# A GAT layer on one core: the row merges of both sorts as odd-even merges, with ends copied by ScalarE

## The chip, the cores and the metric

The kernel runs on one core of one Trainium2 chip. The metric is the device time of one execution in microseconds (us); the time of before is the median of three executions. Engine names are those of the profile: PE is TensorE's matmul side, PEld its weight loads, DVE is VectorE, ACT is ScalarE, POOL is GpSimd, SP is SyncE. L249 is line 249 of the kernel before.

## What is computed

The reference is a graph attention layer with 4096 nodes of 64 features, 50,000 random edges and 4 heads of 64 outputs. Cut to what matters:

```python
x_proj[h] = x @ weight[h]
score[h, e] = leaky_relu(x_proj[h, src[e]] . att_src[h] + x_proj[h, dst[e]] . att_dst[h], 0.2)
output[h, d] = sum over e with dst[e] == d of exp(score[h, e]) * x_proj[h, src[e]]
output[h, d] /= sum over the same e of exp(score[h, e]) + 1e-8
```

## The kernel before, in words

Edges are sorted on the chip so that the gather of source rows and the sums by destination become matmuls with one-hot matrices. The work has four stages.

**Keys.** The edge list arrives by DMA as 128 partitions of 391 columns (padded to L = 512 with a large key). DVE packs source and destination of an edge into one number (L944 to L949). Meanwhile POOL builds small constants (L97 to L178), among them two selector matrices `sel1` (four pieces of 128 columns, L168) and `sel2` (L171), and DVE waits for the first edges.

**First sort.** DVE sorts the rows, `Sorter.rows` (L266): merges of 2, 4, ... 512 columns, merge number k taking k steps. Each step is `Sorter.apart` (L220): compare columns h apart, write minima and maxima into the next of three or four buffers (`sA`, `sB`, `sZ`, `sY`). A step is three instructions: minima of one part of the columns, maxima of all, minima of the other part; the next step can begin on the first part while the last instruction is under way. Columns past 391 are padding, so the small merges work on 384 or 392 columns. Then `Sorter.runs` (L292) merges the rows of a run of four partitions: ACT multiplies by a sign (L301), DVE swaps partitions (L304) and joins (L307, L310), then nine column steps (a "crossing"), a 32 x 32 transposition (`turn`, L285), one or two steps, a transposition back, nine more steps. The result goes to HBM (L338).

During these steps ACT counts edges by source group: 16 passes of Sign with an accumulator (L345), whose sums over partitions PE forms with `sel1` (L355). The counts tell where each group's stretch begins. PE and ACT then prepare tables (`tables`, L485): transposes of x and of the weights, and attention scores of all nodes (L525, 128 small fp32 matmuls). `tables` is a generator; the calls of `next(rest)` decide where in each engine's queue its pieces stand.

**Second sort** (`group`, L452). POOL gathers four stretches per partition by indirect DMA (L445), two for the left 256 columns and two for the right. `Sorter.pairs` (L254) merges each half as soon as it is there, then `rows(9)` merges both into sorted rows of 512, and `runs` merges runs of eight partitions with two turns back and forth. ACT has 32 Sign passes here (L345, 13 of them queued ahead of `runs`, the rest behind the sign multiplication L301 and two casts L469). PE idles, so `busy` (L967) queues filler matmuls of 512 columns on it: one that waits for the 26th count (`WARM`), 12 more (`EARLY`), then the matmul of the counts (L355, `sel2`), which needs all 32, then 34 fillers (`LATER`). Behind them in PE's queue stands `spread` (L594), which copies the sorted fields of a partition to all partitions and which needs DVE's fields (L984, L985) cast by ACT (L986).

**Blocks.** For 32 blocks of 128 destinations: one-hot matrices by DVE (L615, L617), gathers by PE (L634 to L636), exponentials and evictions by ACT (L646, L648), weighted values by DVE (L668), sums by PE (L732), the projection and the store. The first block gets its indices by `spread`, later ones over HBM.

Instructions stand in the order in which the program lists them on each engine (the whole of it is scheduled by hand), so a waiting instruction holds up all that is behind it on its engine. The lines of `group` that fix the order here (the second part is `then`, called by `runs` behind the sign multiplication):

```python
        for f in todo[:SOON]:
            f()
        so.begin(raw)
        so.pairs(5)
        so.rows(9)
        ...
            for f in todo[SOON:]:
                f()
            if between:
                busy(EARLY, (sel2[:], sgn[:, WARM:WARM + 1]))
            st.ps = counts(pp, sgn, 8 * NI, [sel2[:]])
            if between:
                S.copy(out=adb[:, :, 0:P], in_=av(identb[:], 0, [0, ND], [1, P]))
                busy(LATER)
```

Of the kernel before, what the change touches and what calls it, by code (L numbers as in the profile page):

```python
# [11 lines left out]
P = 128  # L12
# [19 lines left out]
SOON = 13  # L32
WARM = 26
EARLY = 12
REST = 2
LATER = 34
# [14 lines left out]
def kernel(ctx: ExitStack, tc: tile.TileContext, x: bass.AP, edge_index: bass.AP,  # L51
# [48 lines left out]
    ident = cst.tile([P, P], F32)  # L100
    make_identity(nc, ident[:])
# [9 lines left out]

# [13 lines left out]
    p8 = bits("p8", 3, 15)  # L125
    p4 = bits("p4", 2, 31)
# [6 lines left out]
    ones = cst.tile([P, 1], F32)  # L133
# [32 lines left out]
    sel1 = cst.tile([P, SETS, P], F32)  # L166
# [3 lines left out]
    sel2 = cst.tile([P, P], F32)  # L170
    G.tensor_scalar(out=sel2[:], in0=av(ioF[:], 0, [0, 8], [1, 16]), scalar1=p8[:, 0:1], scalar2=None,  # L171
                    op0=OP.is_equal)
# [19 lines left out]
    long = cst.tile([P, SPANS], F32)  # L192
# [4 lines left out]
    class Sorter:  # L197


        def __init__(self, pool):  # L200
            self.a = [None, *(pool.tile([P, L], F32, name=n) for n in ("sA", "sB", "sZ", "sY"))]

        def begin(self, first):
            self.a[0] = first
            self.cur = 0

        def step(self, ring=4):
            s = self.a[self.cur]
            self.cur = self.cur % ring + 1
            return s, self.a[self.cur]  # L210
# [9 lines left out]
        def apart(self, j, width=L, cut=L // 2, right=False, at=0, mirror=False, opposed=False, ring=4, to=None, then=None):  # L220


            s, d = self.step(ring)
            d = to or d
# [8 lines left out]
            if right and n > 1:  # L233
                parts.reverse()
            for (o, *dims), op in ((parts[0], OP.min), (whole, OP.max), (parts[1], OP.min)):
                low = at + o
                top = op == OP.max
                if mirror:
                    turned = [*dims[:-1], [-1, dims[-1][1]]]
                    i0 = o % (2 * h)  # L240
                    out = av(d[:], low + h * top, *dims)
                    in0 = av(s[:], low + h * top, *dims)
                    in1 = av(s[:], low - i0 + 2 * h - 1 - i0 - h * top, *turned)
                else:
                    out, in0, in1 = av(d[:], low + h * top, *dims), av(s[:], low, *dims), av(s[:], low + h, *dims)
# [4 lines left out]
                if then:  # L250
                    then()
                    then = None

        def pairs(self, alone):  # L254

            k = 8
            was = self.cur
            for at in (0, L // 2):
                self.cur = was
                self.apart(k - 1, L // 2, at=at, mirror=True)  # L260
                for j in range(k - 2, k - 1 - alone, -1):
                    self.apart(j, L // 2, L // 4, True, at)
            for j in range(k - 1 - alone, -1, -1):
                self.apart(j)

        def rows(self, first, n=L, then=None):  # L266

            w8 = -(-n // 8) * 8
            w128 = n // 128 * 128 if n % 128 <= 8 else L
            for k in range(first, 10):  # L270
                w = w8 if k <= 3 else w128 if k <= 7 else L
                if k <= 7:
                    for j in range(k - 1, -1, -1):
                        self.apart(j, w, 256 if k == 7 else 192, mirror=j == k - 1, ring=3, then=then)
                        then = None
                        if k == 4 and j == 2 and w < w8:
                            V.tensor_copy(out=self.a[1][:, w:w8], in_=self.a[3][:, w:w8])
                else:
                    self.apart(k - 1, w, mirror=True)
                    for j in range(k - 2, -1, -1):  # L280
                        self.apart(j, w if j > 6 else w128 if j > 2 else w8, right=k == 9)
                if k == 7:
                    assert self.cur == 1

        def turn(self, parts):  # L285

            s, d = self.step()
            w = L // parts
            for i in reversed(range(parts)):
                V.transpose(out=d[:, i * w:(i + 1) * w], in_=s[:, i * w:(i + 1) * w])  # L290

        def runs(self, size, then, skey, to=None, fine=0, between=()):  # L292
# [6 lines left out]
            halves = (slice(L // 2, L), slice(0, L // 2))  # L299
            for c in halves:  # L300
                S.activation(out=y[:, c], in_=s[:, c], func=ACTF.Identity, scale=sig[:, 0:1])  # L301
            then()
            for c in reversed(halves):
                V.stream_shuffle(out=z[:, c], in_=s[:, c], mask=[p ^ 1 for p in range(32)])  # L304
            d = self.step()[1]
            for c in halves:
                V.scalar_tensor_tensor(out=d[:, c], in0=av(z[:], L - 1 - c.start, [-1, L // 2]), scalar=sig[:, 0:1],  # L307
                                       in1=y[:, c], op0=OP.mult, op1=OP.min)
            s, d = self.step()
            V.tensor_scalar(out=d[:], in0=s[:], scalar1=sj[0][:, 0:1], scalar2=None, op0=OP.mult)  # L310
            for m in range(1, levels):
                for j in range(8, -1, -1):
                    self.apart(j, right=True)
                self.turn(2)
                self.apart(m, right=True, opposed=True)
                for j in range(m - 1, -1, -1):
                    self.apart(j, right=True)
                self.turn(1)
            todo = list(between)
            for j in range(8, fine, -1):  # L320
# [3 lines left out]
                else:  # L324
                    self.apart(j, right=True)
# [776 lines left out]
```

## Time and profile before

| | |
|---|---|
| median of three executions | 259.68 us (259.49, 259.68, 260.8) |
| the profiled execution, its own time | 260.12 us |
| its span in the trace | 258.2 us |
| busy: PE / DVE / ACT / POOL | 201.1 / 242.4 / 200.0 / 48.7 us |
| first instruction to the end of the first sort's row steps | 0 to 35.4 us |
| crossings and turns of the first sort | 35.4 to 54.0 us |
| through HBM to the second sort | 54.0 to 60.7 us |
| second sort | 60.7 to 102.9 us |
| blocks | 102.9 to 258.2 us |

In a row of the timeline stand the start of the first instruction in us, the time from its start to the end of the last of the row, the engine, the line, the operation, what it writes and reads with shapes, and the number of instructions; in brackets, the idle time before it and what ended it. Instructions of DVE overlap a little at their ends, so what one costs in a stream is read from start to start. "span" is from the first instruction to the last; the execution's own time is 1.9 us more.

### The profile page before, as it was taken

How to read it: one execution, taken by the hardware profiler on the slowest of the kernel's cores; microseconds unless marked ns; L12 is line 12 of the kernel's file. 1: busy time of each engine (PE TensorE's matmuls, PEld its weight loads, DVE VectorE, ACT ScalarE, POOL GpSimd, SP SyncE). 2: the span in 40 equal slices, each digit the busy share in tenths (PEclk: the TensorE clock that was granted, in tenths of full speed). 3: DMA queues.
4: the chain of work that ended last, by engine and by line, in shares of the span. 5: the costliest groups of instructions: out<-in, count | busy, mean ns of one | idle time of the engine just before them, and what ended most of it. 6: DMA issues, size and time to landing. Idle time of an engine off the chain costs nothing.

```text
span 258.2 us, 6892 instructions
## 1 busy us (share of the span) xinstructions
PE 201.1 (78%) x2541; PEld 178.9 (69%) x2541; DVE 242.4 (94%) x674; ACT 200.0 (77%) x514; POOL 48.7 (19%) x102
## 2 busy tenths in 40 slices
PE   0003569999300499778999999999999999999994
PEld 0003339999200245567999999999999999999994
DVE  5999999955999999889999999999999999999992
ACT  2970681002999983898999999999999999999981
POOL 7898700014000000455000006600000000000000
PEclk9999995555555579999999999999999999999998
DMA  4013000011000000269777877687866868776011
GB/s 124 1 32 142 10 1 3 0 41 41 1 1 0 0 3 0 63 232 400 302 286 253 298 232 294 251 302 260 279 255 227 324 226 322 250 279 238 25 43 67
DMA packets 12422, 39.43 MB, mean 153 GB/s; under 512 B 2208, under 2 KB 7904, under 8 KB 8800
## 3 DMA queue, kind: packets, MB, share of 16 engines
q1 hardware_dynamic: 10752, 36.84, 39.2%
q10 hardware_dynamic: 928, 1.51, 1.8%
q0 software_dynamic: 704, 0.59, 1.0%
q8 instruction: 21, 0.34, 0.5%
q14 instruction: 17, 0.14, 0.2%
HBM read 33.96 MB, written 4.98 MB: 151 GB/s over the span
## 4 chain that ended last, share of the span: by engine, by line
PE 57%; DVE 24%; ACT 10%; DMA 5%; issue 2%; POOL 1%; DVEq 0%; SPq 0%; POOLq 0%; ACTq 0%
PE acc L732 20%; PE ps L635 10%; ACT junk L345 8%; PE ps L636 6%; PE ps L634 6%; PE pt L827 5%; DVE sB L249 5%; PE warm L973 5%; DVE sZ L249 5%; DVE sA L249 5%; PE pt L812 3%; DVE sY L249 2%; DMA bc<-gat_bins 1%; DVE oh L615 1%; DVE val L668 1%
## 5 line engine op out<-in xcount | busy, mean ns | idle before, releaser
L648 ACT CAST xs<-ps 128x1176 bf16<-128x1176 f32 (+1 forms) x96 | 103.6, 1083 | 0.0
L668 DVE TENSOR_TENSOR val<-xs,val 128x3072 bf16<-128x3072 bf16 (+2 forms) x64 | 75.1, 1174 | 0.7
L732 PE MATMUL acc<-val,xs 128*128 128x264 bf16 x496 | 66.4, 276 | 1.0 <-PE ps L636 1.0
L634 PE MATMUL ps<-xa,oh 128*128 128x68 bf16 x512 | 51.7, 194 | 2.2 <-ACT xs L648 1.3
L732 PEld LDWEIGHTS <-xs 128*128 128x128 bf16 x496 | 46.2, 98 | 7.0 <-issue 1.1
L635 PE MATMUL ps<-adb,oh 128*128 128x132 bf16 x512 | 49.6, 220 | 0.0
L634 PEld LDWEIGHTS <-oh 128*128 128x128 bf16 x512 | 43.8, 97 | 2.0 <-DVE oh L615 0.9
L635 PEld LDWEIGHTS <-oh 128*128 128x128 bf16 x512 | 40.8, 97 | 3.2 <-issue 2.5
L615 DVE TENSOR_SCALAR oh<-bc,pF 128x3328 bf16<-128x3328 bf16 (+4 forms) x38 | 36.1, 951 | 0.8 <-ACT bc L602 0.4
L636 PE MATMUL ps<-xa,oh 128*128 128x68 bf16 x512 | 36.3, 194 | 0.4 <-DVE oh L617 0.4
L646 ACT ACTIVATE ex<-ps 128x48 bf16<-128x48 f32 (+1 forms) x192 | 33.2, 248 | 3.5 <-PE ps L635 1.0
L636 PEld LDWEIGHTS <-oh 128*128 128x128 bf16 x512 | 28.6, 97 | 0.9 <-DVE oh L617 0.5
L525 PEld LDWEIGHTS scores<-uv,xT 64*128 64x128 f32 x128 | 27.6, 318 | 0.4 <-issue 0.4
L525 PE MATMUL scores<-uv,xT 64*128 64x4 f32 x128 | 27.7, 353 | 0.0
L345 ACT ACTIVATE junk<-kr,nb 128x512 f32<-128x512 f32 x32 | 23.1, 722 | 1.4 <-ACT kr L457 0.4
L249 DVE TENSOR_TENSOR sB<-sA 128x128 f32<-128x128 f32 (+6 forms) x90 | 22.7, 308 | 0.1
L617 DVE TENSOR_SCALAR oh<-bc,pF 128x1664 bf16<-128x1664 bf16 (+4 forms) x38 | 22.3, 588 | 0.0
L249 DVE TENSOR_TENSOR sZ<-sB 128x128 f32<-128x128 f32 (+7 forms) x87 | 21.8, 306 | 0.1
L355 PE MATMUL cnt_ps<-sgn,sel 128*128 128x17 f32 (+1 forms) x10 | 2.4, 368 | 21.3 <-POOL attbd L494 21.3
L827 PE MATMUL pt<-Wbd,aT 128*128 128x128 f32 x124 | 19.0, 275 | 0.0
L457 ACT ACTIVATE kr<-raw,goff 128x256 f32<-128x256 f32 x2 | 1.0, 508 | 22.7 <-DMA raw<-gat_sorted,wi 22.7
L355 PEld LDWEIGHTS cnt_ps<-sgn,sel 128*128 128x128 f32 x10 | 2.5, 329 | 21.7 <-POOL attbd L494 21.3
(173 smaller groups left out, 310.9 us busy)
## 6 DMA issues: line engine op xcount, KB each, us to landing
bc<-gat_bins SPq DMA_DIRECT2D x28, 1024.0 KB, 5.9
out_dram<-res SPq DMA_DIRECT2D x32, 128.0 KB, 2.6
xf<-in_x_dram ACTq DMA_DIRECT2D x1, 1024.0 KB
bc<-gat_bins SPq DMA_DIRECT2D x1, 768.0 KB, 6.1
bc<-gat_bins SPq DMA_DIRECT2D x1, 640.0 KB
bc<-gat_bins SPq DMA_DIRECT2D x1, 384.0 KB, 3.7
gat_sorted<-sY SPq DMA_DIRECT2D x2, 128.0 KB, 1.7
gat_sorted<-ki SPq DMA_DIRECT2D x2, 128.0 KB, 1.7
```

The source lines that it names most:

```text
L249: V.tensor_tensor(out=out, in0=in0, in1=in1, op=op)
L345: todo = [lambda b=b: S.activation(out=junk[:], in_=v, func=ACTF.Sign, bias=nbnd[:, b:b + 1], scale=1.0, accum_out=sgn[:, b:b + 1]) for b ...
L525: T.matmul(out=scores[:, k * NB + b, :], lhsT=nodes(b), rhs=uv[:, k, :], start=(k == 0 and b == 0), stop=True, skip_group_check=True)
L615: V.tensor_scalar(out=av(oh[:], *e), in0=av(bc[:], *e), scalar1=pF[:, 0:1], scalar2=None, op0=OP.is_equal)
L634: kinds = [lambda i, t, **how: T.matmul(out=ps[:, i, P:P + XC], lhsT=hot(2 * t + 1), rhs=xa[:, t, :], **how), lambda i, t, **how: T.matmul ...
L635: lambda i, t, **how: T.matmul(out=ps[:, i, 0:S0], lhsT=hot(2 * t), rhs=adb[:, b, :], **how),
L636: lambda i, t, **how: T.matmul(out=ps[:, i, P:P + XC], lhsT=hot(2 * NT + t), rhs=xa[:, NR + t, :], **how)]
L646: S.activation(out=av(ex[:], 2 * (k * H * NT + t0), [2, n], [2 * NT, H], [1, 2]), in_=av(ps[:], P, [PW, n], [1, H], [0, 2]), func=ACTF.Exp ...
L648: S.copy(out=xs[:, t0:t0 + n, 0:P + XC], in_=ps[:, 0:n, 0:P + XC])
L668: V.tensor_tensor(out=av(val, t0 * AW, [VW, H * n], [1, Din]), in0=av(xs, S0 + t0 * XW, [XW, n], [0, H], [1, Din]), in1=av(val, t0 * AW + ...
L732: T.matmul(out=acc[:, 0:AW], lhsT=xs[:, t, 0:P], rhs=val[:, t, :], start=(t == 0), stop=(t == NT - 1), **how)
L827: T.matmul(out=self.pt[:, k * P:(k + 1) * P], lhsT=self.aT[b][:, k * P:(k + 1) * P], rhs=Wbd[:, k, :], start=True, stop=True, skip_group_c ...
```

## The change

It does six things. (1) A merge of 2^k sorted columns becomes an odd-even merge (`merge`): its first step compares all pairs n/2 apart, each later step only the inner columns, so the outer columns of every later step need no comparison. They must stand in both buffers between which the later steps alternate, so the first step writes inner columns into one buffer and outer ones into another, and ACT copies the outermost eighths into the third; step 4 is the first that reads that copy (in the merge of 8 columns, the next merge). The four buffers become parts of one tile. Merges of 2 and 4 become `fours`, ten instructions on four contiguous quarters. Merge 8 of the first sort stays as it was. (2) `wide` does the same for the second sort, with ACT's Sign passes handed out in groups of 4, 5 and 23 between the copies. (3) Crossings and turns work in parts of 384 and 128 columns in place of 256 and 256, or 512. (4) `sel1` and `sel2` are built by DVE behind the padding memsets, in place of POOL. (5) The pieces of `tables` and the 16 Sign passes of the first sort are handed out between the merges; the copies into `xa` and `adb` move to the first sort's end. (6) `WARM`, `EARLY`, `LATER` are 25, 28, 17 in place of 26, 12, 34; `ones` and `long` become bf16.

The diff, cut to its core:

```diff
+PARTS = (slice(L // 4, L), slice(0, L // 4))
-SOON = 13
-WARM = 26
-EARLY = 12
-LATER = 34
+WARM = 25
+EARLY = 28
+LATER = 17
...
+    p4 = bits("p4", 2, 31)
+    p8 = bits("p8", 3, 15)
+    ident = cst.tile([P, P], F32)
+    make_identity(nc, ident[:])
...
-    for i in range(SETS):
-        G.tensor_scalar(out=sel1[:, i, :], in0=av(ioF[:], 8 * i, [0, 16], [1, 8]), scalar1=p4[:, 0:1], scalar2=None,
-                        op0=OP.is_equal)
-    G.tensor_scalar(out=sel2[:], in0=av(ioF[:], 0, [0, 8], [1, 16]), scalar1=p8[:, 0:1], scalar2=None,
...
+            bufs = pool.tile([P, 4, L], F32, name="sorted")
+            self.a = [None, *(bufs[:, i, :] for i in range(4))]
...
+        def merge(self, k, at=0, ns=1, left=0, top=L, way=None, steps=(1, 9), meanwhile=()):
+            n = 1 << k
+            q, third = n // 4, n // 8
+            one, two, three = way or ((self.cur + i) % 4 + 1 for i in range(3))
+            segs = ((left, ns), (0, left)) if left else ((0, 1),)
...
+            for i in range(max(steps[0], 1), min(steps[1], k) + 1):
+                h = n >> i
+                if i == 1:
+                    s, d, apart = self.a[self.cur], self.a[one], (one - two) * L
...
+                        compare(s, d, OP.min, at + q, at + 3 * q, [1, q])
...
+                            compare(s, d, OP.max, at, at + h, [q, 2], [1, q], out=av(d, at + h, [q - apart, 2], [1, q]))
+                        compare(s, self.a[two], OP.min, at, at + h, [1, q])
+                    if k > 2:
+                        ends = 1 if top < at + n else 2
+                        e = (at, [n, ns], [n - third, ends], [1, third])
+                        S.copy(out=av(self.a[three], *e), in_=av(self.a[two], *e))
+                    for f in meanwhile:
+                        f()
+                    self.cur = one
+                    continue
+                s, self.cur = self.a[self.cur], three if i % 2 else two
+                d = self.a[self.cur]
+                m = min((1 << (i - 1)) - 1, -(-(top - at - h) // (2 * h)))
...
+                    c = 1 << (i - 3)
+                    pairs(OP.min, 0, 1, 0, c)
+                    pairs(OP.max, 0, 1, 0, m)
+                    pairs(OP.min, 0, 1, c, m)
...
+        def wide(self, alone, load, between, meanwhile):
+            k = 8
+            way = 1, 2, 3
+            for at in (0, L // 2):
+                self.cur = 0
+                load(at)
+                self.merge(k, at, way=way, steps=(1, alone))
+            between()
...
+            self.merge(9, meanwhile=meanwhile)
...
+            self.fours(w8 // 4, then)
+            for k in range(3, 8):
+                w = w8 if k <= 3 else w128
+                self.merge(k, 0, w >> k, 2 if k == 7 else 192 >> k, meanwhile=meanwhile[k],
+                           way=ways[k])
+            self.apart(7, mirror=True, right=True)
+            for j in range(6, -1, -1):
+                self.apart(j, w128 if j > 2 else w8, 128, right=True)
+            self.merge(9, top=w8, meanwhile=meanwhile[9])
...
+            for c in PARTS:
+                V.transpose(out=d[:, c], in_=s[:, c])
...
+        so.wide(6, load, lambda: count(4), [lambda: count(5)])
...
-            for f in todo[SOON:]:
-                f()
+            count(len(todo))
...
-                S.copy(out=adb[:, :, 0:P], in_=av(identb[:], 0, [0, ND], [1, P]))
...
+    V.memset(av(so.a[1], EL, [L, 4], [1, L - EL]), KPAD)
+    V.tensor_scalar(out=sel1[:], in0=av(ioF[:], 0, [8, SETS], [0, 16], [1, 8]), scalar1=p4[:, 0:1], scalar2=None,
+                    op0=OP.is_equal)
+    V.tensor_scalar(out=sel2[:], in0=av(ioF[:], 0, [0, 8], [1, 16]), scalar1=p8[:, 0:1], scalar2=None, op0=OP.is_equal)
...
+    passes(4)
+    so.rows(EL, right[4], {3: (lambda: passes(1),), 4: (lambda: passes(2),), 5: (lambda: passes(3),),
+                           6: (lambda: passes(3), more), 7: (lambda: passes(len(todo)), count, more, blocks.clear),
+                           9: (more,)})
+    so.runs(RUN1, more, skey1)
```

## Rows read from the trace of the kernel before

**Rows 1.** Page: busy tenths of DVE and TensorE's granted clock in 40 slices.
```profile
DVE  5999999955999999889999999999999999999992
PEclk9999995555555579999999999999999999999998
```
**Rows 2.** Page: the chain that ended last, share of the span by line.
```profile
PE acc L732 20%; PE ps L635 10%; ACT junk L345 8%; PE ps L636 6%; PE ps L634 6%; PE pt L827 5%; DVE sB L249 5%; PE warm L973 5%; DVE sZ L249 5%; DVE sA L249 5%; PE pt L812 3%; DVE sY L249 2%; DMA bc<-gat_bins 1%; DVE oh L615 1%; DVE val L668 1%
```
**Rows 3.** Timeline of ACT, second sort: sign multiplication, Sign passes, cast of the fields.
```profile
75.06 0.89 ACT L301 ACTIVATE sZ<-sA,sig 128x256 f32<-128x256 f32 x2
...
76.16 0.72 ACT L345 ACTIVATE junk<-kr,nb 128x512 f32<-128x512 f32 x1
...
77.00 0.72 ACT L345 ACTIVATE junk<-kr,nb 128x512 f32<-128x512 f32 x1
...
99.82 0.41 ACT L986 CAST tb<-t 128x256 bf16<-128x256 int32 x1 [4.11 <-DVE t L985]
```
**Rows 4.** Timeline of PE around its fillers, second sort.
```profile
87.63 5.28 PE L973 MATMUL warm<-identb 128*128 128x512 bf16 x12
...
92.99 7.52 PE L973 MATMUL warm<-identb 128*128 128x512 bf16 x34
100.35 1.47 PE L600 MATMUL ps<-tb,identb 128*128 128x256 bf16 x12
```
**Rows 5.** Timeline of DVE, first sort: row steps of 384 columns, end of rows, crossing steps of 512.
```profile
6.95 0.54 DVE L249 TENSOR_TENSOR sA<-key 128x196 f32<-128x196 f32 x2
...
17.09 0.68 DVE L249 TENSOR_TENSOR sB<-sA 128x96 f32<-128x96 f32 x3
17.70 0.68 DVE L249 TENSOR_TENSOR sZ<-sB 128x96 f32<-128x96 f32 x3
...
34.76 0.70 DVE L249 TENSOR_TENSOR sB<-sA 128x68 f32<-128x68 f32 x3
...
37.60 0.83 DVE L249 TENSOR_TENSOR sZ<-sB 128x128 f32<-128x128 f32 x3
38.34 0.82 DVE L249 TENSOR_TENSOR sY<-sZ 128x128 f32<-128x128 f32 x3
```
**Rows 6.** Timeline of DVE around a transposition of 512 columns.
```profile
45.65 0.82 DVE L249 TENSOR_TENSOR sB<-sA 128x128 f32<-128x128 f32 x3
46.51 0.71 DVE L290 STREAM_TRANSPOSE sZ<-sB 128x512 f32<-128x512 f32 x1
47.26 0.83 DVE L249 TENSOR_TENSOR sY<-sZ 128x128 f32<-128x128 f32 x3
```
**Rows 7.** Timeline of POOL while it builds selectors.
```profile
12.36 2.76 POOL L168 TENSOR_SCALAR sel<-ioF,p_f 128x128 f32<-128x128 f32 x4
```
**Rows 8.** Timeline of DVE in that stretch, row steps of 384 columns.
```profile
14.49 0.77 DVE L249 TENSOR_TENSOR sA<-sZ 128x96 f32<-128x96 f32 x3
15.18 0.78 DVE L249 TENSOR_TENSOR sB<-sA 128x96 f32<-128x96 f32 x3
```
**Rows 9.** Timeline of ACT: a small copy, of 64 columns.
```profile
26.26 0.21 ACT L508 COPY wT<-lent 128x64 f32<-128x64 f32 x1
```
**Rows 10.** Timeline of DVE: the wait for the first edges.
```profile
3.89 0.26 DVE L944 TENSOR_SCALAR sli<-eS 128x196 int32<-128x196 int32 x1 [1.54 <-DMA eS<-in_edge_index_dram]
```
**Rows 11.** Timeline of DVE, second sort: first half, second half, last row step.
```profile
60.71 0.56 DVE L249 TENSOR_TENSOR sA<-raw 128x64 f32<-128x64 f32 x3 [5.45 <-DMA raw<-gat_sorted,wi]
...
63.23 0.56 DVE L249 TENSOR_TENSOR sA<-raw 128x64 f32<-128x64 f32 x3
...
73.86 0.82 DVE L249 TENSOR_TENSOR sA<-sY 128x128 f32<-128x128 f32 x3
```
**Rows 12.** Timeline of DVE: the count read, the fields for `spread`.
```profile
97.77 0.19 DVE L386 TENSOR_SCALAR cnt<-cnt_ps 128x33 f32<-128x33 f32 x1
...
99.56 0.22 DVE L985 TENSOR_SCALAR t<-kb 128x128 int32<-128x128 int32 x1
```
**Rows 13.** Timeline of POOL: issue of the fourth part of the gather.
```profile
60.65 0.94 POOL L445 DMA_INDIRECT raw<-gat_sorted,wi  x1 [0.30 <-issue]
```

More of the change, by code (lines that the diff above doesn't have):

```diff
@@ L132 @@
     G.memset(eps[:], 1e-8)
-    ones = cst.tile([P, 1], F32)
+    ones = cst.tile([P, 1], BF16)
     G.memset(ones[:], 1.0)
@@ L191 @@
     SPANS = SETS + NI + (2 * NI << FINE)
-    long = cst.tile([P, SPANS], F32)
+    long = cst.tile([P, SPANS], BF16)
     rows = cst.tile([1, SPANS], F32)
@@ L256, in pairs @@
+        def wide(self, alone, load, between, meanwhile):
             k = 8
-            was = self.cur
+            way = 1, 2, 3
             for at in (0, L // 2):
[L259 to L283, printed above, removed]
@@ L287, in turn, with cross @@
+        def turn(self):
             s, d = self.step()
-            w = L // parts
-            for i in reversed(range(parts)):
-                V.transpose(out=d[:, i * w:(i + 1) * w], in_=s[:, i * w:(i + 1) * w])
+            for c in PARTS:
+                V.transpose(out=d[:, c], in_=s[:, c])
+        def cross(self, j, **how):
+            self.apart(j, cut=L // 2 if j == 7 else L // 4, right=True, **how)
         def runs(self, size, then, skey, to=None, fine=0, between=()):
@@ L324, in runs @@
                 else:
[L325 removed]
+                    self.cross(j)
             s, d = self.step()
@@ L511, in tables @@
             S.copy(out=uv[:, :, 2 * i:2 * i + 2], in_=av(ps2[:], 0, [2, 2], [1, 2]))
-        S.copy(out=xa[:, :, H:XC], in_=xf[:])
         xT = pr.tile([Din, N], F32)
@@ L955, with passes @@
         V.tensor_scalar(out=sli[:, E0:EL], in0=sli[:, E0:EL], scalar1=float(NR), scalar2=None, op0=OP.min)
-    for f in (*right[2:4], *todo):
+    for f in right[2:4]:
         f()
-    cps = counts(few, sgn, NR, [sel1[:, i, :] for i in range(SETS)])
     rest = tables(pr, Lent(blocks.psx, "ps"), scores)
-    next(rest)
-    blocks.clear()
-    so.rows(1, EL, right[4])
-    so.runs(RUN1, lambda: next(rest, None), skey1)
-    bounds(so1, cps)
+    more = lambda: next(rest, None)
+    def passes(n):
+        for f in todo[:n]:
+            f()
+        del todo[:n]
+    passes(4)
+    cps = []
+    count = lambda: cps.append(counts(few, sgn, NR, [sel1[:, i, :] for i in range(SETS)]))
+    so.rows(EL, right[4], {3: (lambda: passes(1),), 4: (lambda: passes(2),), 5: (lambda: passes(3),),
+                           6: (lambda: passes(3), more), 7: (lambda: passes(len(todo)), count, more, blocks.clear),
+                           9: (more,)})
+    so.runs(RUN1, more, skey1)
+    bounds(so1, cps[0])
     with first as st:
```

144 lines of the change are left out of this document (98 added, 46 removed).

## The prediction

> **What bounds the kernel now.** I read the page's slices first [rows 1]: DVE is busy without a break from the keys to the end of the second sort but for two waits on DMAs, and TensorE's granted clock falls to half in the sort and is whole again from the 15th slice on. The chain by line [rows 2] says why this matters: over half of it is the block stage (L732, L634 to L636), which the change leaves alone, so whatever the sorts save arrives as an earlier start of the blocks, or not at all. It also has an entry that is no DVE work: ACT's Sign passes (L345) and PE's fillers (L973). That is the second thing to see. At the end of the second sort two chains arrive together: DVE's fields are cast by ACT until 99.82 + 0.41 = 100.23 [rows 3], and the last filler gives PE free for `spread` at 100.35 [rows 4]. A change that only makes DVE faster would be stopped by the fillers, and these start when ACT has reached the count they wait for.
>
> **What a DVE step costs.** A step of three instructions takes 0.61 us on 384 columns and 0.74 on 512, from start to start [rows 5]. 1.04 ns a column and 0.069 us an instruction give both (0.40 + 0.21; 0.53 + 0.21). An instruction that needs the result of the one just before it waits some 0.11 us longer: that is the step before the transposition, 0.86 in place of 0.74 [rows 6].
>
> **First sort, rows.** Before: from 6.95 to 34.76 + 0.61 = 35.37 [rows 5]. The program lists 135 instructions on 17,672 columns there, 18.4 + 9.3 = 27.7; 28.4 are measured. Of the difference some 0.45 stands in the stretch where POOL builds the selectors [rows 7]: five steps of 384 columns take 0.70 [rows 8] in place of 0.61. After, counted from the diff: `fours` 10 instructions on 980 columns; merge of 8, 10 on 882; merges of 16 to 128, 66 on 7,002 (each step i over 1 - 2^(1-i) of the columns); merge 8 unchanged, 24 on 3,224; merge 9, 27 on 3,360. Sum 137 on 15,448: 16.1 + 9.4 = 25.5, plus 0.27 for the second half of the keys in between (195 columns). It starts 0.56 ahead of 6.95, at 6.39, where before the first part of merge 1 stood, so it ends at 32.2: **3.2 us** gained, of which 2.3 are columns not compared, 0.45 POOL's, the rest copies and waits.
>
> Of POOL's selectors the trace shows the price: 0.09 us of DVE for each of five POOL instructions of 0.69 [rows 7, 8]. [...]
>
> **What the rows' gain needs.** ACT must deliver six copies in time. A copy of 64 columns takes 0.21 [rows 9], one of 98 to 128 then 0.24 to 0.26. From the end of step 1 to the start of step 4 DVE has two steps of its own, half and three quarters of the columns: 0.40 + 0.50 = 0.9 us for 384 columns. Copy and two hand-overs take about 0.45, so each has some 0.4 to spare if ACT is free; the passes handed out between (1, 2, 3, 3, 3 of 0.75) fill less than the merges they lie beside. The moved DMA issues and table copies stand behind the copy of merge 7 and are done by about 25; that of merge 9 is wanted at 27.5. Bounds: no wait, or the rival below.
>
> **First sort, the rest.** Joins: 34.76 + 0.61 to 37.60 is 2.23 [rows 5]; in parts, 512 columns each for shuffle and join and half the time for the multiplication, six instructions, two waits and a late start of ACT: 1.97, so 0.25 gained. A transposition of 512 and the wait before it: 0.12 + 0.75 [rows 6]; in two parts 0.53 + 0.14, no wait: 0.2 gained. Crossing steps have the same columns and instructions: nothing. Sum of the first sort 3.65; with small waits that I don't see I take **3.5**. Selectors and longer memsets on DVE: 363 more padding columns (0.38 at 1.04 ns), 512 (0.53) and 128 (0.13) columns and instructions, some 1.2 us, in an idle wait of 1.54 for the edges [rows 10]; without that cover they would cost the 1.2.
>
> **Second sort.** All is 3.5 earlier; in times of before: DVE starts at 60.71, the second half arrives at 63.23, rows end at 73.86 + 0.74 = 74.60 [rows 11]. After: a half is 17 instructions on 1,288 columns, 2.51, so the first half ends at 63.22, just as the second arrives; that ends at 65.74; two common steps 6 on 1,012, 1.47; merge 9, 26 on 4,098, 6.06 and a wait of 0.11: 73.4. Gain 1.2. Here ACT's order decides. The sign multiplication started at 75.06 because ACT was in its 13th pass [rows 3]; now only 9 passes are ahead and it starts as rows end, 73.4 + 0.15 - 3.5 = 70.05. Then 1.1 us for it and the casts (75.06 to 76.16), and 16 passes of 0.845 (76.16 to 77.00) [rows 3] to the 25th count: 71.15 + 13.5 = 84.65. Before: 76.16 + 13 x 0.845 = 87.15, and the first filler at 87.63 [rows 4]. So the **fillers start 2.5 us earlier**, not 4.7: ACT idles ahead of the copy of merge 9 and ahead of the multiplication, and does four passes fewer there.
>
> **The end of the second sort.** 46 fillers and the counts took 87.63 to 100.35 [rows 4]. Now 45: one of 0.22 less, if the clock rises as long after the first filler as before. `spread` starts at 100.35 - 2.5 - 0.2 = 97.65. Is DVE late? Its count read stood at 97.77 [rows 12]; it now comes there at 97.77 - 3.5 - 1.2 - 0.25 - 2 x 0.2 = 92.4. But the counts' matmul now stands behind 28 fillers, not 12. At half clock a filler takes 5.28/12 = 0.43 with its tail, at full clock 7.52/34 = 0.22 [rows 4]; the rise lay 5.4 us after the first filler. So 12.6 slow and 15.4 fast ones, 85.15 + 5.4 + 3.3 = 93.9, the counts 0.3 more: DVE waits nearly 2 us. From the count read to the cast fields it is 100.23 - 97.77 = 2.46 [rows 3, 12], so they are there at 96.7, ahead of the last filler by 1. **PE's fillers end last, and the gain is 2.7 of DVE's 5.3.** What follows (evictions, one-hots, gathers of the first blocks) moves with it. The bf16 check sum replaces two small matmuls among the blocks: nothing. The rest of ACT's moved copies lie where ACT idled.
>
> The profiled execution took 260.12; minus 2.7 is 257.4. It lay 0.44 above the median of 259.68, so for a median I say **257.0**.
>
> **Rivals.** (a) *The fillers let go earlier.* If the clock rises at the first filler, 45 take 9.7 and the counts 0.3: `spread` could start at 95.2, DVE's fields are there at 94.9. Gain 5.1, 254.5. For: the fillers start at another time, and the rise needn't keep its distance; each us that it comes earlier gives 0.5. Against: in the one rise that the trace has, TensorE was busy for 5 us before it. (b) *Small or no gain.* The clock rises 2.7 us later (-1.35), or three or four copies come 0.3 late (-1): 258 to 259.5. For: the spare time of a copy is 0.4 us and less in the merge of 8. (c) *Slower: each merge waits for its copy at once.* If the wait is put on the whole of the new common tile, not on the columns, step 2 already waits: 0.08 until the writes end, 0.1 to ACT, 0.24, 0.07 back, 0.49 in each of nine merges, 4.4 in all against 2.7: 261.4. It decides from 0.3 us a merge on. Against: a wait by columns is what the trace shows, DVE began on the left half of `raw` at 60.71 [rows 11] while the gather of its fourth part had just been issued [rows 13]. For: these regions are interleaved, and that is not shown. (d) *The columns aren't the cost.* Were a step paid by instructions, 137 against 135 would gain nothing; [rows 5] exclude it, as 384 and 512 columns cost 0.61 and 0.74.
>
> **How the numbers follow.** Chances: forecast (gain 1.9 to 3.5) 0.5, (a) 0.18, (b) 0.22, (c) 0.1, (d) none. No change within 0.5% is 258.4 to 261.0, about what a measurement of this kernel can tell; half of (b) and a little of (c) lie there: 0.14. Slower 0.08, faster 0.78. The range reaches to all but the ends of (a) and (b): 254.8 to 259.4. The forecast's own is 256.2 to 257.8.
>
> **What would show it.** Right: first sort's rows ending near 32 and the stores 3.5 earlier; steps with fewer columns, no idle of DVE behind ACT's copies; steps of 0.61 where POOL built; the first filler near 85; DVE idle ahead of L386 for 1 to 2 us, released by PE; `spread` right behind the last filler. Wrong: DVE idle before step 2 or 4 of a merge, released by ACT (c, b); the fillers ending before the fields (a); or a gain of DVE below 4 us.

## The result, and the profile after

The changed kernel takes 257.75 us (median of 4 runs, 257.2 to 257.86), the kernel before beside it 260.24 (4 runs): ratio 0.9899, 95% interval 0.986 to 0.9939. 257.0 was predicted. The profiled execution has a span of 255.9 us, that of before 258.2. On another chip the gain was a third of this; that is told with the third set of experiments.

The page: busy tenths of VectorE, TensorE's granted clock in 40 slices, and the chain that ended last by line. The clock falls and rises as in [rows 1]; the Sign passes (L422 here) have gone from 8% of the chain to 5%.

```profile
DVE  7999999928999978989999999999999999999993
PEclk9999985555555589999999999999999999999999
PE acc L816 20%; DVE sorted L253 11%; PE ps L719 10%; DVE sorted L240 7%; PE ps L720 6%; PE ps L718 6%; PE pt L911 5%; ACT junk L422 5%; PE warm L1071 5%; PE pt L896 3%; DMA bc<-gat_bins 2%; DVE oh L699 1%; DVE val L752 1%; DMA eS<-in_edge_index_dram 1%; ACT bc L686 1%
```

The timeline of VectorE (start, length, line and operation, count, and in brackets the idle time ahead of it with what seems to have ended it):

```profile
3.85 0.26 DVE L1033 TENSOR_SCALAR sli<-eS 128x196 int32<-128x196 int32 x1 [0.74 <-DMA eS<-in_edge_index_dram]
...
6.38 0.25 DVE L328 TENSOR_TENSOR sorted<-key 128x98 f32<-128x98 f32 x1
...
8.40 3.36 DVE L253 TENSOR_TENSOR sorted<-sorted 128x98 f32<-128x98 f32 x19
12.17 10.68 DVE L253 TENSOR_TENSOR sorted<-sorted 128x84 f32<-128x84 f32 x57 [0.41 <-ACT junk L422]
...
27.76 5.45 DVE L253 TENSOR_TENSOR sorted<-sorted 128x128 f32<-128x128 f32 x27
...
35.28 0.82 DVE L240 TENSOR_TENSOR sorted<-sorted 128x128 f32<-128x128 f32 x3
...
44.75 5.95 DVE L240 TENSOR_TENSOR sorted<-sorted 128x128 f32<-128x128 f32 x24
...
58.25 0.56 DVE L253 TENSOR_TENSOR sorted<-raw 128x64 f32<-128x64 f32 x3 [5.54 <-DMA raw<-gat_sorted,wi]
...
65.11 6.15 DVE L253 TENSOR_TENSOR sorted<-sorted 128x128 f32<-128x128 f32 x26
...
95.09 0.19 DVE L463 TENSOR_SCALAR cnt<-cnt_ps 128x33 f32<-128x33 f32 x1 [1.25 <-PE cnt_ps L432]
...
105.84 0.22 DVE L628 TENSOR_SCALAR t<-win 128x128 int32<-128x128 int32 x1
...
112.50 0.55 DVE L699 TENSOR_SCALAR oh<-bc,pF 128x1248 bf16<-128x1248 bf16 x1 [0.71 <-DMA bc<-gat_bins]
```

The wait for the edges is 0.74 instead of 1.54 [rows 10]: the selectors lie in it. Crossings start at 35.28 instead of 37.60 [rows 5], the steps behind the second turn at 44.75 instead of 47.26 [rows 6], the second sort at 58.25 instead of 60.71 [rows 11]. One wait was not foreseen: 0.41 in the merge of 16. At the end VectorE waits 1.25 for the counts.

ScalarE's timeline, second sort and the first block's exponentials:

```profile
71.30 0.91 ACT L376 ACTIVATE sorted<-sorted,sig 128x384 f32<-128x384 f32 x2 [0.92 <-DVE sorted L253]
...
72.42 0.73 ACT L422 ACTIVATE junk<-kr,nb 128x512 f32<-128x512 f32 x1
...
97.12 0.41 ACT L1084 CAST tb<-t 128x256 bf16<-128x256 int32 x1 [5.25 <-DVE t L1083]
...
104.45 0.35 ACT L730 ACTIVATE ex<-ps 128x48 bf16<-128x48 f32 x2
```

TensorE's timeline around the fillers:

```profile
86.44 8.47 PE L1071 MATMUL warm<-identb 128*128 128x512 bf16 x28
94.75 0.30 PE L432 MATMUL cnt_ps<-sgn,sel 128*128 128x33 f32 x2
94.97 3.83 PE L1071 MATMUL warm<-identb 128*128 128x512 bf16 x17
98.63 1.47 PE L684 MATMUL ps<-tb,identb 128*128 128x256 bf16 x12
```

The fields are cast at 97.12 + 0.41 = 97.53 and wait 1.1 us for the last filler. VectorE's row merges of the second sort end 3.4 us earlier (65.11 + 6.15 against 73.86 + 0.82 [rows 11]), and ScalarE's sign multiplication behind them starts 3.8 earlier (71.30 against 75.06 [rows 3]). Of this 1.2 are left at the first filler (86.44 against 87.63 [rows 4]), 1.7 at `spread` (98.63 against 100.35), and 2.5 in the total.

### The profile page after: what moved, and what is told of

Its sections match the earlier page's. It is cut to its first block, busy times and chain, and to the rows that moved or that the text cites. A ratio compares the mean times of both kernels' runs of the same rounds, so it can differ in the third digit from the quotient of the medians.

```text
span 255.9 us, 6908 instructions
## 1 busy us (share of the span) xinstructions
PE 200.9 (79%) x2539; PEld 178.4 (70%) x2539; DVE 238.9 (93%) x682; ACT 201.8 (79%) x523; POOL 44.7 (17%) x97
## 4 chain that ended last, share of the span: by engine, by line
PE 57%; DVE 27%; ACT 7%; DMA 5%; issue 2%; POOL 0%; DVEq 0%; SPq 0%; POOLq 0%; ACTq 0%
PE acc L816 20%; DVE sorted L253 11%; PE ps L719 10%; DVE sorted L240 7%; PE ps L720 6%; PE ps L718 6%; PE pt L911 5%; ACT junk L422 5%; PE warm L1071 5%; PE pt L896 3%; DMA bc<-gat_bins 2%; DVE oh L699 1%; DVE val L752 1%; DMA eS<-in_edge_index_dram 1%; ACT bc L686 1%
## 5 line engine op out<-in xcount | busy, mean ns | idle before, releaser
L732 ACT CAST xs<-ps 128x1176 bf16<-128x1176 f32 (+1 forms) x96 | 103.2, 1076 | 0.0
L720 PE MATMUL ps<-xa,oh 128*128 128x68 bf16 x512 | 36.3, 194 | 0.4 <-DVE oh L701 0.4
L240 DVE TENSOR_TENSOR sorted<-sorted 128x192 f32<-128x192 f32 (+2 forms) x141 | 34.4, 326 | 0.0
L253 DVE TENSOR_TENSOR sorted<-sorted 128x128 f32<-128x128 f32 (+22 forms) x157 | 30.1, 270 | 0.4 <-ACT junk L422 0.4
L720 PEld LDWEIGHTS <-oh 128*128 128x128 bf16 x512 | 28.6, 97 | 0.9 <-DVE oh L701 0.5
L422 ACT ACTIVATE junk<-kr,nb 128x512 f32<-128x512 f32 x32 | 23.1, 722 | 0.9
L1069 PE MATMUL warm<-sgn,sel 128*128 128x1 f32 x2 | 0.6, 364 | 20.4 <-ACT junk L422 20.4
```

The source lines that it names most:

```text
L240: V.tensor_tensor(out=out, in0=in0, in1=in1, op=op)
L253: V.tensor_tensor(out=out, in0=av(s, lower, *dims), in1=av(s, upper, *dims), op=op)
L422: todo = [lambda b=b: S.activation(out=junk[:], in_=v, func=ACTF.Sign, bias=nbnd[:, b:b + 1], scale=1.0, accum_out=sgn[:, b:b + 1]) for b ...
L720: lambda i, t, **how: T.matmul(out=ps[:, i, P:P + XC], lhsT=hot(2 * NT + t), rhs=xa[:, NR + t, :], **how)]
L732: S.copy(out=xs[:, t0:t0 + n, 0:P + XC], in_=ps[:, 0:n, 0:P + XC])
```

## The experiments

Stated before any ran: Theory A, the fillers end last and set the end. Theory B, fillers and the chain through memory (counts, key store, gather of windows, their bins, third selection) end together, so that a gain on one is lost on the other. Rival D, VectorE's own work sets the end. Three sets ran on three chips, with the kernel before beside each: 260.26, 259.88 and 259.99. The changed kernel itself ran beside the third set only. In the first set its time is the 257.75 of the result, so differences of a few tenths from it are not shown there.

### First set: what binds behind the second sort

**12 fillers behind the counts in place of 17.**

```
-LATER = 17
+LATER = 12
```

> One edit: 12 fillers instead of 17 behind the second sort's counts. Theory A (the fillers end last and set the end): the last filler ends 5 x 0.22 = 1.1 us sooner, the spread starts at about 97.6 instead of 98.63 (the fields are there at 97.53), and the kernel gains about 1.0 us, to 256.7. Theory B (fillers and the chain through memory end together: counts, key store, gather of windows, its bins, the third selection): the spread starts 1.0 earlier, but VectorE then waits as much longer for the bins' load ahead of the third selection (0.71 now, about 1.5 then), and the kernel gains 0.2 us or less.

Measured: 256.73 us, ratio 0.9857 (0.9835 to 0.988), 1.0 below the changed kernel. TensorE's and VectorE's timelines:

```profile
94.87 2.75 PE L1071 MATMUL warm<-identb 128*128 128x512 bf16 x12
97.48 1.47 PE L684 MATMUL ps<-tb,identb 128*128 128x256 bf16 x12
```

```profile
105.40 0.28 DVE L628 TENSOR_SCALAR t<-win 128x128 int32<-128x128 int32 x1 [0.58 <-DMA win<-gat_sorted,to]
...
111.88 0.56 DVE L699 TENSOR_SCALAR oh<-bc,pF 128x1248 bf16<-128x1248 bf16 x1 [0.50 <-DMA bc<-gat_bins]
```

`spread` is 1.15 earlier, as A and B both say; then VectorE waits 0.58 for the windows, where it did not wait, and its unpacking is 0.44 earlier, the third selection 0.62. In the two profiles 0.7 reaches the end. That is between A (1.0) and B (0.2), and nearer to A.

**22 fillers ahead of the counts in place of 28.**

```
-EARLY = 28
+EARLY = 22
```

> One edit: 22 fillers instead of 28 ahead of the second sort's counts, 17 behind as now. Theories A and B alike: the clock still rises about 4.6 us after the first filler, since TensorE stays busy; the counts come 6 x 0.22 = 1.3 us sooner, VectorE's wait for them (1.25) is all but gone, and the spread (bound by the fillers) and the key store (bound by VectorE) both come 1.0 to 1.3 sooner: a gain of 1.0 to 1.3 us, to about 256.6. If the wait for the counts does not bind (Theory C: the chain through memory hangs on something other than VectorE's sort end), the gain is under 0.3.

Measured: 257.02 us, ratio 0.9877 (0.9855 to 0.9899), 0.7 below. VectorE's timeline, then TensorE's granted clock by stretches (the columns after the bounds: length, busy time of PE, PEld, DVE, ACT, POOL, clock, DMA share, GB/s):

```profile
93.84 0.18 DVE L463 TENSOR_SCALAR cnt<-cnt_ps 128x33 f32<-128x33 f32 x1
...
104.49 0.23 DVE L628 TENSOR_SCALAR t<-win 128x128 int32<-128x128 int32 x1 [0.25 <-DMA win<-gat_sorted,to]
...
113.48 0.56 DVE L699 TENSOR_SCALAR oh<-bc,pF 128x1248 bf16<-128x1248 bf16 x1 [0.49 <-DMA bc<-gat_bins]
```

```profile
112.00:116.00 4.00, 2.78 (x39) 2.60 (x39) 3.37 (x7) 3.33 (x12) 2.71 (x8) 0.76 1.01 407
116.00:120.00 4.00, 4.00 (x55) 3.49 (x54) 3.86 (x7) 2.90 (x9) 0.75 (x1) 0.81 1.02 392
```

The counts are read 1.25 earlier without a wait and `spread` starts at 96.95, 1.7 earlier. Part is handed back among the first blocks, where VectorE waits 0.49 for the next bins. The clock falls there too, but is not shown to cost anything: this execution took 256.98, and the three others, with a mean granted clock of 1.0, took 256.93 to 257.36. Fewer fillers ahead of the counts help, by less than the 1.0 expected.

**The old fillers in the changed kernel.**

```
-WARM = 25
-EARLY = 28
+WARM = 26
+EARLY = 12
...
-LATER = 17
+LATER = 34
```

> The three filler constants as before the change (first filler behind the 26th sign pass, 12 ahead of the counts, 34 behind), all else changed. The counts are then bound by the 32nd pass alone (91.87): VectorE reads them about 1.2 us sooner and waits for nothing there; the first filler comes 0.85 later and the last one at about 100.0, so the spread starts 1.4 later than the 98.63 of now. Theory A (the fillers set the end): 1.0 to 1.4 us slower, about 259. Theory B (both chains): between 0.5 faster and 0.8 slower, with VectorE's wait ahead of the first selections longer and the wait for the bins' load gone.

Measured: 258.4 us, ratio 0.9932 (0.9914 to 0.995), 0.65 slower than the changed kernel. TensorE's timeline and VectorE's:

```profile
99.60 1.47 PE L684 MATMUL ps<-tb,identb 128*128 128x256 bf16 x12
```

```profile
101.93 0.62 DVE L699 TENSOR_SCALAR oh<-bc,pF 128x1536 bf16<-128x1536 bf16 x1 [2.78 <-ACT bc L686]
```

The counts are read at 93.85, but `spread` starts at 99.60, and VectorE idles 2.78 us ahead of its first selection; the wait for the bins (0.71) is then gone. That is B: 1.0 lost at `spread`, 0.2 in this profile's span, 0.65 in the medians. Against before, all of the sorts' work thus gives 1.9 us. The rest of the 2.5, some 0.6, would be the new filler numbers'; the intervals of the two ratios overlap, so its size is not shown.

**VectorE given 1.2 us more to do behind the second sort's rows.**

```
             then()
+            if size == 8:
+                for i in range(2):
+                    V.tensor_tensor(out=spare[:], in0=s[:], in1=s[:], op=OP.min)
```

> One addition: two comparisons of 512 columns (0.60 us each, 1.2 in all, into a tile that nothing reads) on VectorE right behind the second sort's row merges. Theories A and B: VectorE's wait for the counts (1.25) takes them up, cnt is read at the same time, and the kernel changes by 0.2 us or less. Rival D (VectorE's own work sets the end): 1.0 to 1.2 us slower.

Measured: 258.06 us, ratio 0.9916 (0.9897 to 0.9934), 0.3 above the changed kernel. VectorE's timeline:

```profile
95.36 0.19 DVE L466 TENSOR_SCALAR cnt<-cnt_ps 128x33 f32<-128x33 f32 x1
```

VectorE is 1.46 us later just ahead of the counts (the comparisons before them start at 94.54 against 93.08). It reads the counts at 95.36 with almost no wait ahead (0.06), and is 0.27 later from there to the end. So nearly all of the added work cost nothing, and Rival D falls: behind 71 us the change's gain on VectorE was worth nothing either.

### Second set: what the first sort's rows lost

The rows and joins, from the first comparison to the first crossing, take 35.28 - 6.38 = 28.90 us in the changed kernel. This sum is compared below, since the start itself moves by 0.2 with the edges. The whole times of this set are not compared with 257.75: the changed kernel did not run on this chip, and the third set shows that the chip matters. Theory W: the wait of 0.41 is ScalarE's copy, signalled late. Rival F: it belongs to VectorE's own instructions at that place.

**No passes behind the copy of the merge of 16.**

```
-4: (lambda: passes(2),), 5: (lambda: passes(3),)
+4: (), 5: (lambda: passes(5),)
```

> The two Sign passes that ScalarE runs behind its copy in the merge of 16 are moved behind its copy in the merge of 32 (five there); nothing else. Theory W (VectorE's 0.41 us wait ahead of step 4 of the merge of 16 is the copy's signal, held up by the passes queued with it on ScalarE): the wait there is gone, the row merges end 0.4 to 0.5 us sooner; a wait of at most as much may appear ahead of step 4 of the merge of 64, whose copy now stands behind five passes. Rival F (the wait belongs to VectorE's instructions at that place, not to ScalarE): it stays at 0.41.

Measured: 259.63 us, ratio 0.9994 (0.9973 to 1.0015); first sort 29.32. VectorE's timeline:

```profile
12.14 4.98 DVE L253 TENSOR_TENSOR sorted<-sorted 128x84 f32<-128x84 f32 x27 [0.40 <-DVE sorted L253]
17.55 5.72 DVE L253 TENSOR_TENSOR sorted<-sorted 128x84 f32<-128x84 f32 x30 [0.43 <-ACT sorted L282]
```

The first wait stays, with no pass queued behind the copy of this merge: it is not the passes. The second stands ahead of step 4 of the merge of 64 and is put down to the copy (L282), which is really late there, as foreseen. Its 0.43 is what the first sort is longer, 29.32 against 28.90.

**The ends copied by VectorE.**

```
-                        S.copy(out=av(self.a[three], *e), in_=av(self.a[two], *e))
+                        V.tensor_copy(out=av(self.a[three], *e), in_=av(self.a[two], *e))
```

> The ends of the merges are copied by VectorE itself, in place of ScalarE. In the first sort 98, 4 x 96 and 64 columns: at 1.04 ns a column and 0.069 us an instruction 0.57 + 0.41 = 1.0 us more on VectorE, 0.7 if a plain copy runs at two columns a cycle; the 0.41 us wait ahead of step 4 of the merge of 16 and the small ones of 0.05 go if they belong to ScalarE's hand-over (Theory W), so the crossing starts 0.2 to 0.5 us later than 35.28; if the 0.41 stays (Rival F), 0.7 to 1.0 later. In the second sort 64 + 64 + 128 columns cost 0.4 to 0.5, which the wait for the counts covers. In all 0.2 to 1.0 us slower.

Measured: 260.33 us, ratio 1.0014 (0.9991 to 1.0038); first sort 29.69, 0.79 longer though no wait of 0.41 is left. So neither theory has both: the wait goes as W says, the crossing is as late as F says. Counted against the changed kernel without its wait, the copies cost 1.2: six of 0.11 to 0.16 from start to start (9.18 to 9.34 the first, 29.08 to 29.19 the last), 0.80 together and so between the 0.7 and the 1.0 expected, and the rest ahead of them for the step just before (the first starts 0.04 behind the end of the comparisons, 9.14, where in the changed kernel comparisons in a row start 0.08 ahead of it). On ScalarE they save 0.8 as measured, 1.2 by that count.

**The selectors back on GpSimd.**

```
-    V.tensor_scalar(out=sel1[:], in0=av(ioF[:], 0, [8, SETS], [0, 16], [1, 8]), scalar1=p4[:, 0:1], scalar2=None,
-                    op0=OP.is_equal)
+    for i in range(SETS):
+        G.tensor_scalar(out=sel1[:, i, :], in0=av(ioF[:], 8 * i, [0, 16], [1, 8]), scalar1=p4[:, 0:1], scalar2=None,
+                        op0=OP.is_equal)
...
-    V.tensor_scalar(out=sel2[:], in0=av
+    G.tensor_scalar(out=sel2[:], in0=av
```

> The five selector instructions go back to GpSimd, behind its other constants, as they were before the change; nothing else. By the rows of the kernel before (steps of 384 columns 0.70 in place of 0.61 beside them) the row merges of the first sort take 0.45 us longer, and the two VectorE instructions no longer stand ahead of the keys, where they were covered. [...]

Measured: 259.1 us, ratio 0.9968 (0.995 to 0.9985); first sort 29.10. GpSimd's timeline and VectorE's:

```profile
14.92 2.94 POOL L1024 TENSOR_SCALAR sel<-ioF,p_f 128x128 f32<-128x128 f32 x4
17.84 0.67 POOL L1027 TENSOR_SCALAR sel<-ioF,p_f 128x128 f32<-128x128 f32 x1
```

```profile
8.49 14.64 DVE L253 TENSOR_TENSOR sorted<-sorted 128x98 f32<-128x98 f32 x76
```

The 0.41 is gone from the merges: they are one group of 76 now. With neither selectors nor wait the same 76 take 14.00 (below), so GpSimd's 3.6 us of selectors cost VectorE at most 0.64. The rows of before said 0.45.

**Equal halves in joins, turns and crossings.**

```
-PARTS = (slice(L // 4, L), slice(0, L // 4))
+PARTS = (slice(L // 2, L), slice(0, L // 2))
...
-        self.apart(j, cut=L // 2 if j == 7 else L // 4, right=True, **how)
+        self.apart(j, cut=L // 2, right=True, **how)
```

> Joins, multiplications, turns and crossings in parts of 256 and 256 columns again in place of 384 and 128; nothing else. By the sum of the prediction the turns keep their parts, so all that comes back is the wait between the two parts: a second part that needs the first one's results waits 0.11 longer wherever the last part is too short to cover it. I expect 0 to 0.3 us on VectorE in the first sort and nothing at the end of the kernel beyond 0.2.

Measured: 259.21 us, ratio 0.9968 (0.9941 to 0.9995). The first sort to the first crossing takes 28.92, to the steps behind the second turn 38.52 in place of 38.37: the uneven parts are worth 0.15 us there, as foreseen.

### Third set: the place of the wait, and a better kernel

**The changed kernel as it is.**

> The changed kernel as it is, once more, as the measure for the others of this call. If the chip of the second call (where four kernels stood 1 to 2 us above what their edits cost, all with ScalarE idle for 2.0 us longer ahead of its second pair of exponentials at about 104.5) is what made them slow, this kernel is as slow there: 259 to 260 where that idle shows, 257.7 where it does not. If it was the edits, it is 257.7 on any chip.

Measured: 259.22 us (12 runs, 257.76 to 260.24), ratio 0.9962 (0.994 to 0.9983). So on this chip it is not an edit that makes the kernel slow. Up to 106 us VectorE is within 0.25 us of the first profile, `spread` starts at 98.86; then ScalarE's and VectorE's timelines read:

```profile
103.66 1.15 ACT L732 CAST xs<-ps 128x1176 bf16<-128x1176 f32 x1
106.67 0.31 ACT L730 ACTIVATE ex<-ps 128x48 bf16<-128x48 f32 x2 [1.86 <-PE ps L720]
```

```profile
111.06 0.55 DVE L699 TENSOR_SCALAR oh<-bc,pF 128x1248 bf16<-128x1248 bf16 x1 [1.16 <-ACT bc L686]
```

In the first profile of this kernel these exponentials follow the copy at once (104.45, above). Here ScalarE idles 1.86 us ahead of them, and the end is 1.8 later. All four kernels of the second set show 1.83 to 1.85 at the same instruction, none of the first set does. What it waits for the trace does not say beyond the name of TensorE's L720, and no run was made that would tell.

The idle is half of the loss. Two runs of the second set have it alike, but not the granted clock (ScalarE's timeline, then the stretches with columns as above; first no passes behind the copy of the merge of 16, then equal halves):

```profile
106.36 0.31 ACT L730 ACTIVATE ex<-ps 128x48 bf16<-128x48 f32 x2 [1.85 <-PE ps L720]
...
109.00:110.00 1.00, 1.00 (x7) 0.71 (x5) 0.58 (x1) 0.39 (x2) 0.00 (x0) 0.50 0.44 83
```

```profile
105.79 0.31 ACT L730 ACTIVATE ex<-ps 128x48 bf16<-128x48 f32 x2 [1.84 <-PE ps L720]
...
109.00:110.00 1.00, 1.00 (x11) 0.78 (x9) 0.26 (x2) 1.00 (x2) 0.00 (x0) 1.00 0.67 203
```

From `spread` to the end of the span the first profile of the changed kernel takes 157.3 us, the kernel here 158.8. From the exponentials behind the idle to the end it is 150.2 and 150.3 with the idle alone (equal halves, ends by VectorE). With the idle and then a stretch of the clock at half (0.50 from 108 to 111 us with no passes behind the copy, from 109 to 111 with the selectors on GpSimd) it is 151.0 and 150.9. The kernel here and the four memsets below take 151.0 too, at mean granted clocks of 0.887 and 0.993, and are counted with these. So of the 1.5 us some 0.75 goes with the idle and as much again with the clock; no edit tried either apart. The kernel before meets something like it: in the second and third sets 4 of its 51 executions have a mean granted clock of 0.993, as the profile with four memsets has, and they take 261.56 to 261.78, the others 259.5 to 261.21.

**Four memsets of one column ahead of the keys.**

```
+    for i in range(4):
+        few0 = cst.tile([P, 1], F32, name=f"few0{i}")
+        V.memset(few0[:], 0.0)
```

> Four memsets of one column each (0.06 us) on VectorE behind the selectors, in its idle wait for the edges, where they cost nothing by themselves. Rival F (the 0.41 us wait in the merge of 16 belongs to a place in VectorE's instruction stream, its 63rd instruction): the wait comes four instructions sooner in the work, ahead of the last part of step 2, is longer by the 0.5 us that VectorE needs for those four (0.9 to 1.0), and is gone ahead of step 4; the crossing starts 0.3 to 0.5 later. Theory W (ScalarE's copy is late for step 4): the wait stays ahead of step 4 at 0.4, the crossing at 35.3.

Measured: 259.27 us, ratio 0.9952 (0.993 to 0.9974); first sort 34.91 - 6.46 = 28.45. VectorE's timeline:

```profile
8.48 14.00 DVE L253 TENSOR_TENSOR sorted<-sorted 128x98 f32<-128x98 f32 x76
```

Both theories fall: the wait neither stays nor grows, it is gone. W is out by this and by the second set: ScalarE's copy is the same. That leaves VectorE's stream, as F said, but not F's law.

**15 fillers ahead of the counts, 19 behind.**

```
-EARLY = 28
+EARLY = 15
...
-LATER = 17
+LATER = 19
```

> 15 fillers ahead of the second sort's counts in place of 28, 19 behind them in place of 17: the counts wait for the last sign pass alone and the last filler ends about when the fields are there. VectorE reads the counts at about 93.9 without a wait, the spread starts at about 96.4 (98.63 before), the key store is 1.2 earlier; from there the chain through memory (windows, bins) bounds, so of the 2.2 us at the spread 0.8 to 1.2 reach the end: 256.5 to 257.0 on a chip where the changed kernel takes 257.7. If TensorE's clock falls among the first blocks, as it did with 22 fillers, 0.3 of it is lost.

Measured: 256.16 us (5 runs, 255.82 to 256.59), ratio 0.9837 (0.9811 to 0.9863): 3.1 below the changed kernel on this chip. TensorE's and ScalarE's timelines:

```profile
92.43 4.26 PE L1071 MATMUL warm<-identb 128*128 128x512 bf16 x19
96.52 1.47 PE L684 MATMUL ps<-tb,identb 128*128 128x256 bf16 x12
```

```profile
102.34 0.35 ACT L730 ACTIVATE ex<-ps 128x48 bf16<-128x48 f32 x2
...
105.82 0.29 ACT L730 ACTIVATE ex<-ps 128x32 bf16<-128x32 f32 x2 [2.10 <-PE ps L684]
```

That is also below the 256.5 to 257.0 expected. `spread` is 2.3 us earlier than beside it, the counts are read at 93.73 without a wait. ScalarE's idle of 2 us stands one pair of exponentials later, and the clock does not fall among the first blocks (its mean is 1.0). From `spread` to the end it takes 158.3 us where the changed kernel beside it takes 158.8, so part of the 3.1 is the clock's fall that is missing here, and not the fillers' own length; it was not tried apart.

**The same, with the second selector built in the wait for the gather.**

```
+    bounds(so1, cps[0])
+    sel2 = cst.tile([P, P], F32)
+    V.tensor_scalar(out=sel2[:], in0=av(ioF[:], 0, [0, 8], [1, 16]), scalar1=p8[:, 0:1], scalar2=None, op0=OP.is_equal)
```

> As the kernel with 15 and 19 fillers, and the second selector is built by VectorE in its wait for the second sort's gather in place of its wait for the edges. By Rival F VectorE's 63rd instruction then stands one comparison later in the work and its wait is 0.2 to 0.25 shorter, so all that follows comes 0.2 sooner than with 15 and 19 fillers alone; by Theory W there is no difference.

Measured: 256.25 us, ratio 0.9852 (0.9826 to 0.9879), no different from 256.16. First sort 28.77, 0.13 shorter; VectorE's timeline:

```profile
12.31 10.53 DVE L253 TENSOR_TENSOR sorted<-sorted 128x168 f32<-128x168 f32 x56 [0.23 <-DVE sorted L253]
```

The wait stands one comparison later in the work and is shorter, as F said here. Both kernels beat the changed one and the one before.

## Why the prediction was right, and where it was not

The mechanism was right: fillers end last, VectorE's gain is mostly stopped there, the gain is a few us. 257.0 was said, 257.75 measured. That the numbers lie so near is partly luck: `spread` came 1.7 us earlier and not 2.7, and 0.6 came back behind it that no step had foreseen. Two of the prediction's own signs of being wrong came up as well. VectorE idles ahead of step 4 of a merge, though the runs show that it does not wait for ScalarE's copy. And VectorE is ready for the counts at 95.09 - 1.25 = 93.84, 3.9 us earlier than before and not 5.3. By its steps:

- *First sort, rows: 3.2 us.* This is the term that failed: 2.2 (the rows end at 27.76 + 5.45 = 33.21, not 32.2). 0.45 of the missing 1.0 is the wait in the merge of 16, shown by the run with four memsets. Without that wait the new rows still take 26.4 (28.45 less 2.03 for the joins) where the sum of columns and instructions is 25.8: I had taken all of the old rows' 0.7 over that sum as removable. 0.13 of the 0.6 is the wait of the last step, which the old rows had too; the rest is spread over many steps, 0.04 ahead of step 4 of the merges of 32 and 64 among them (14.12 to 14.31 and 16.93 to 17.12, where 0.15 lie between such comparisons one step before).
- *GpSimd's 0.45.* At most 0.64 for all five selectors: 14.64 with them on GpSimd against 14.00.
- *The copies come in time.* They do: but for the 0.41, which is not ScalarE's, no wait of more than 0.05 stands ahead of a step of the first sort that reads a copy, unless five passes are queued ahead of the copy (0.43). ScalarE begins a copy 0.03 to 0.10 behind the comparisons before it (9.21 to 9.24, 10.84 to 10.93) and takes 0.24 to 0.37 for it, 0.27 on 96 columns; the 0.07 back to VectorE was an estimate that no trace here shows. Rival (c) did not occur.
- *Joins 0.25, turn 0.2.* The joins gave less, 0.1: 2.03 and a wait of 0.13 are 2.16 in place of 2.23. The turn is right, about 0.2 (the steps behind it are 2.5 earlier where crossings were 2.3). Equal halves cost 0.15 in both together.
- *Selectors hidden in the wait for the edges.* Right: 0.74 of it is left.
- *Second sort's rows 1.2.* 1.0: they end 3.4 earlier, and began 2.5 earlier. The multiplication is 3.8 earlier, since ScalarE's passes no longer hold it up.
- *First filler 2.5 earlier, `spread` 2.7.* 1.2 and 1.7: what the first sort lost, 1.0, came through one to one, and 0.2 of the second sort's rows. From the multiplication to the first filler 15.1 us were predicted, and 86.44 - 71.30 is 15.1.
- *VectorE waits 2 for the counts, fields 1 ahead of the last filler.* 1.25 and 1.1.
- *Clock rise 5.4 after the first filler.* 4.6: TensorE's clock is whole from about 91. With it the fillers and counts took 12.2 us in place of 12.7, not 12.5; rival (a) in small.
- *What follows moves with `spread`.* Not quite: from `spread` to the end of the span it takes 157.3 us instead of 157.9. Two chains meet at the third selection, and a us at `spread` was worth 0.2 to 0.6 at the end in the profiles of the first set (0.97 gave 0.22, 1.15 gave 0.7, 1.68 gave 0.7). The other chain begins with the counts, and those were read 2.7 earlier (95.09 against 97.77 [rows 12]); that this brought the 0.6 is argued and not shown. In the third set ScalarE's idle and the clock's fall took 1.5 away. Neither was in any step of the prediction.
- *Over half of the chain in L732 and L634 to L636.* These four lines of [rows 2] make 42%; the block stage passes half only with its other lines. Nothing in the sum hangs on it.

## What to carry to other kernels

Filler matmuls that stand in a queue with real work were part of the critical path here as soon as the work ahead of them got faster (the fields waited 1.1 us for the last one): size those ahead of a result so that they end when its operands do, and those behind so that they end with the next operands; here that gave more than the sort's whole rewrite on one chip (3.1 us against 0.8), though part of it is a fall of the clock that was missing there. A sum of columns and instructions priced a step well here (0.61 us on 384 columns, 0.74 on 512 [rows 5]), but what the old kernel took beyond that sum stays in the new one unless a row shows what removes it. The gain was 2.5 us on one chip and 0.8 on another: it is to be timed on more than one before its size is believed, and where it differs the granted clock by stretches is to be compared first.

## What was not expected of the hardware

- A wait on VectorE that the profile puts down to ScalarE in some profiles and to VectorE itself in others. In the changed kernel it stands ahead of the 57th instruction that VectorE executes and ends at 12.17 us. In the profiles of this stretch that show it, it ends at 12.14 to 12.31: 0.40 to 0.41 ahead of the first comparison of step 4, and 0.23 ahead of the second with one selector fewer in front, which is the same place in VectorE's stream. With two selectors fewer or four memsets more in front the merges show no wait. What ties it to that place is not shown: the page has a queue that it names instruction (q14), but in the changed kernel the first packet of such a queue inside the span starts at 12.83, 0.66 behind the end of the wait. So what the wait is for, and why four instructions more remove it, is open.
- ScalarE's idle of 1.83 to 1.86 us ahead of one pair of exponentials, on the chips of the second and third sets and not on that of the first; the changed kernel as it is shows it in the third set and not in its first profile. Open.
- TensorE's granted clock falls to half among the first blocks in four of the six profiles of this kernel's filler numbers that have the idle (two show 0.50 from 109 to 111 us, two are counted by their length and mean clock), and 0.75 us of the end goes with it. Why in these four and not in the other two is open.
- TensorE's clock does not always fall in the sort, where it was 0.50 from 38 to 93 us in the profile of before. In 8 of 11 executions of the kernel before in the first set its mean was 0.997 or more, in 3 it was 0.89; the medians are 260.2 and 260.5. So by these the clock's fall in the sort, from which two rivals took their prices, costs the kernel before some 0.3 us.
